# Second expert team's gather spread over the first team's steps from rows with a pool of their own, and router logits in column tiles with a summing product

## Chip, core and metric

One core of a Trainium2 chip. The metric is the device time of one execution in microseconds (us), the median of three runs. The trace is one execution taken by the hardware profiler. Its engines are PE (TensorE matmuls; PEld their weight loads), DVE (VectorE), ACT (ScalarE), POOL (GpSimd) and SP (SyncE, whose queue issues nearly all loads).

## What is computed

A trunk of two layers over 256 positions of width 1024, all in float32. Each layer has four token mixers side by side, then a channel mixer: a dense SwiGLU in layer 0, and in layer 1 eight experts of which each position uses two. The change touches only this last stage:

```python
def moe_ffn(h, router_w, w1, w3, w2):
    logits = (h @ router_w).astype(jnp.float32)
    top_vals, top_idx = lax.top_k(logits, TOP_K)
    top_w = jax.nn.softmax(top_vals, axis=-1)
    gate = jnp.sum(jax.nn.one_hot(top_idx, N_EXPERTS) * top_w[..., None], axis=-2)
    out = jnp.zeros_like(h)
    for e in range(N_EXPERTS):
        out = out + gate[..., e:e + 1] * swiglu(h, w1[e], w3[e], w2[e])
    return out
```

The result goes through a residual sum and a final RMSNorm. The experts' three weight arrays together are 277 MB in float32, and all of it is read.

## The kernel before

A plan is a Python list; `run` (line 192) walks it and emits instructions in its order. A scheduler may then move an instruction ahead of its neighbours on its engine where it waits for nothing, except the matmuls of `tiles` and `warm`, which keep their program order.

**The expert stage.** Experts form two teams of four. Each expert has 64 slots (CAP) for positions, and a team has two reserves of 32 slots, FULL, for experts that are chosen more often. `route` (line 1275) normalises the rows, transposes them into `hT_moe`, multiplies by the router weights `rw` (line 1293: two halves of the positions, eight products each, the stationary operand a 128x128 block of `hT_moe`, the moving one 8 columns), copies the logits to `lg` (line 1295), and finds the two best experts and each position's slot in a chain of small DVE operations. `rows_in_parts` (line 1389) splits the normalised rows into `hh` and `hl`, two float32r parts. `gather(s)` (line 1444) then makes the team's input `X` by multiplying the parts with a 0/1 matrix `pm`: eight chunks of four matmuls (line 1454) for the 256 slots, and `gather_extra` (line 1461) eight chunks of four narrow matmuls (line 1468) for the reserves.

**Weights come in steps.** One step is one k (128 rows of a weight matrix) of four experts: a 2 MB load (1.5 MB for the last columns) into a tile named `quad`. A team has 70 steps: for each of three column blocks (`COLS`) eight of w1 and eight of w3, then 22 of w2. `use` and `round_` (line 1530) consume a step with five calls of `tiles` (line 315), each call four products that stand in four 32-column tiles of the PE array; the first four calls read the `quad`, the fifth reads `own`, a copy of two experts' weights that DVE and ACT make (lines 1526, 1527). In the trace each float32 product is two MATMUL records, so a step is 40 of them.

**Buffers.** Loads are issued on SP's queue in order, each when a place is free. There are four places "A", opened during the last projection of the mixers, one "B", opened when the expert stage begins, and two "first" (FIRST), which are used once and not given back. The five others are given back when their step has been read. So the first seven steps are loaded ahead; load 7 waits for step 0 (load 8 for step 1, and so on to load 11 for step 4), and load 12 waits for step 7, as steps 5 and 6 used the "first" places. (Steps and loads are counted from 0.)

**Side work.** Generators (`Side`, line 126) emit pieces of other work between the calls of `tiles`. What a generator yields sets how long it waits: 1500 units times the number, or 700 for 0, on a planner's count `now` (`tick`, line 253) that each call of `tiles` raises by 858. `finish` steps all active generators until the named one has ended. After step 6 `then` (line 1646) frees the "first" places, makes the second team's `pm`, and starts its gather (`both(1)`, which yields 0 between chunks) and `spread(0)` (line 1476: 12 matmuls of one column, three pairs of transposes). The tiles `hh` and `hl` use four of the five buffers of the tag "g" in the stage's own pool; `silu` (line 1567) needs two of these for the first team's activations. So `use` ends the second team's gather in step 7 (`finish(st["gather", 1])`), before the first `silu`, and then starts `spread(1)`.

Of the kernel before, what the change touches and what calls it, by code (L numbers as in the profile page):

```python
# [10 lines left out]
F32 = mybir.dt.float32  # L11
F32R = mybir.dt.float32r
# [128 lines left out]
class Trunk:  # L141
# [218 lines left out]
    def load_tables(self):  # L360
        nc, a = self.nc, self.a
        n0 = C_OFFS["ident"][1]
        nc.sync.dma_start(self.keep[:, n0:], a["consts"][:, n0:C_KEEP])
        nc.sync.dma_start(self.mixk[:, :C_LATE - C_KEEP], a["consts"][:, C_KEEP:C_LATE])
        rows = self.mixc.tile([102, P], F32, name="rows")
        r = lambda n, pat: a[n].rearrange(pat, p=P)
        nc.sync.dma_start(rows[0:48], r("ssd_conv_w", "l k (b p) -> (l k b) p"))
        nc.sync.dma_start(rows[48:60], r("ssd_conv_b", "l (b p) -> (l b) p"))
        nc.sync.dma_start(rows[60:92], r("ml_conv_w", "l k (b p) -> (l k b) p"))
        nc.sync.dma_start(rows[92:100], r("ml_conv_b", "l (b p) -> (l b) p"))  # L370
        nc.sync.dma_start(rows[100:102], r("gla_b_alpha", "l (b p) -> (l b) p"))
        self.bc = self.mixc.tile([P, 5, L, 4], F32, name="bc")
        for i, n in enumerate(("ssd_dt_bias", "ml_b_i", "ml_b_f", "ssd_a_log", "ssd_d")):
            nc.sync.dma_start(self.bc[:, i], _bcast(a[n], [[4, L], [1, 4]]))
        self.walpha = self.mixc.tile([16, L, P], F32, name="walpha")
        nc.sync.dma_start(self.walpha, a["gla_w_alpha"].rearrange("l r c -> r l c"))
        self.rows = rows
        self.ranks = self.const.tile([P, 2 * P], F32R, name="ranks")
        for i, n in enumerate(("tris", "ones")):
            nc.gpsimd.tensor_scalar(self.ranks[:, i * P:(i + 1) * P], self.c(n), 1.0, None, op0=OP.mult)  # L380
        self.rw = self.const.tile([P, KT, NE], F32, name="rw")
        nc.sync.dma_start(self.rw, a["router_w"][0].rearrange("(k p) e -> p k e", p=P))

    def load_narrow(self, l):

# [889 lines left out]
    def route(self, l):  # L1275
# [8 lines left out]
        self.load_gain("final_norm_g", 0)  # L1284
        hT = early("hT_moe").rearrange("p (k s) -> p k s", k=KT)
        self.turned(h, lambda q, t, pt: nc.scalar.activation(hT[:, q, t], pt, AF.Copy))
        self.rows_in_parts(h)
        nc.scalar.dma_start(self.kept.rearrange("p (a d) -> p a d", a=2), h)
        pl = self.psum()
        lg = T((P, 2, NE), "lg")  # L1290
        for t in range(2):
            for k in range(KT):
                nc.tensor.matmul(pl[:, t * NE:(t + 1) * NE], hT[:, k, t * P:(t + 1) * P], self.rw[:, k],
                                 start=k == 0, stop=k == KT - 1)
        nc.vector.tensor_copy(lg, pl[:, :2 * NE].rearrange("p (t e) -> p t e", t=2))
        self.warm(6)


# [87 lines left out]
            pool.tensor_tensor(gate, ohs[0], ohs[1], op=OP.add)  # L1386
        self.later = later

    def rows_in_parts(self, h):

        self.hh, self.hl = [[self.mp.tile([P, D], F32R, tag="g", bufs=GS, name=f"{n}{self.num()}")
                             for _ in range(2)] for n in ("hh", "hl")]
        for t in range(2):
            self.nc.scalar.activation(self.hh[t], h[:, t], AF.Copy)
            (self.nc.vector, self.nc.gpsimd)[t].tensor_tensor(self.hl[t], h[:, t], self.hh[t].bitcast(F32),
                                                              op=OP.subtract)

    def experts(self, l, n, first):
# [42 lines left out]
                                            st["zo"][:, t, :, s, None].to_broadcast([P, FULL, SUB]),  # L1441
                                            iota[:, None, 1:1 + SUB].to_broadcast([P, FULL, SUB]), op=OP.is_equal)

        def gather(s):

            pm = st["pm", s]
            X = st["X", s] = T((P, KT, WIDE), f"X{s}", pool=self.late if s else self.mp)
            rows = [(self.hh[0], 0), (self.hh[1], 1), (self.hl[0], 0), (self.hl[1], 1)]
            yield 1
            for k in range(KT):  # L1450
                pt = self.psum((P, SLOTS))
                ks = slice(k * P, (k + 1) * P)
                for i, (src, t) in enumerate(rows):
                    nc.tensor.matmul(pt, src[:, ks], pm[:, t, :SLOTS], start=i == 0, stop=i == 3)  # L1454
                yield 0
                if k % 2:
                    nc.vector.tensor_copy(X[:, k, :SLOTS], pt)
                else:
                    nc.scalar.activation(X[:, k, :SLOTS], pt, AF.Copy)

        def gather_extra(s):
            pm, X = st["pm", s], st["X", s]
            rows = [(self.hh[0], 0), (self.hh[1], 1), (self.hl[0], 0), (self.hl[1], 1)]
            pt = self.psum((P, KT, FULL * SUB))
            for k in range(KT):
                ks = slice(k * P, (k + 1) * P)
                for i, (src, t) in enumerate(rows):
                    nc.tensor.matmul(pt[:, k], src[:, ks], pm[:, t, SLOTS:WIDE], start=i == 0, stop=i == 3)  # L1468
                yield 0
            nc.vector.tensor_copy(X[:, :, SLOTS:], pt)  # L1470

        def both(s):
            yield from gather(s)
            yield from gather_extra(s)

        def spread(s):

# [62 lines left out]
        def up(s, ci):  # L1540
            c0, n_ = COLS[ci]
            w_2 = n_ // 2
            got = {}

            def use(w_, k, raw):
                if k == 0:
                    if w_ + ci == 0:
                        self.finish(st["gather", s])
                    got[w_] = {key: self.psum()[:, :w_2] for key in
                               [(h, r) for h in range(2) for r in range(ROUNDS)] + ["full"]}  # L1550
                round_(got[w_], st["X", s][:, k], raw, pick(s, raw, n_), w_2, k == 0, k == KT - 1)
                if k == KT - 1:
                    if s + ci + w_ == 0:
                        self.finish(st["gather", 1])
                        go("spread", 1, spread(1))
                    st["act", s, ci, w_] = sd = Side((silu, act)[w_](s, ci, got))
                    self.spawn(sd)
            return [Step(w[k, :, s * TEAM:(s + 1) * TEAM, c0:c0 + n_], n_, lambda raw, w_=w_, k=k: use(w_, k, raw))
                    for w_, w in enumerate((w1, w3)) for k in range(KT)]
# [13 lines left out]
        def act(s, ci, got):  # L1573
            w = COLS[ci][1] // 2
            nb = w // P
            gT = st["gT", s, ci] = T((P, 8, WIDE), "gT", 3, pool=self.late)
            for key, gv in halves(s, ci):
                nc.vector.tensor_mul(gv, gv, got[1][key])
            for key, gv in halves(s, ci):
# [55 lines left out]
        def go(name, s, gen):  # L1635
            st[name, s] = sd = Side(gen)
            self.spawn(sd)
# [8 lines left out]
        def then():  # L1646
            if first:
                self.early.close()
                self.late = self.pool("late")
            hot(1)  # L1650
            hot_extra(1)
            go("gather", 1, both(1))
            go("spread", 0, spread(0))

        for s in range(TEAMS):
            for ci in range(len(COLS)):
                steps = up(s, ci)
                if s + ci == 0:
                    at = WEIGHTS + 1 + FIRST
                    steps.insert(at, then)  # L1660
                plan += steps
            plan.append(lambda s=s: self.finish(st["spread", s]))
            if s == 0 and n == 0:
                plan.append(self.shares_left)
            plan += down(s)
        return plan

    def moe(self, l):
        def begin():
            self.cutting.close()  # L1670
            self.homes["B"] = self.pool("quad", side="right"), 1
            self.mp = self.pool("moe")
            self.early = ExitStack()
            self.soon = self.pool("soon", ctx=self.early)
            self.homes["first"] = self.soon, FIRST
            self.places.extend(["B"] + ["first"] * FIRST)
        return self.experts(l, 0, [begin, "fetch", lambda: self.route(l)])

    def shares_left(self):

# [4 lines left out]
    def moe_rest(self, l, n=1):  # L1685

        most = self.nc.values_load(self.shares[n - 1]["most"][0:1, 0:1], min_val=0, max_val=S)
        with self.tc.If(most > 0):
            self.nc.vector.tensor_tensor(self.slot, self.slot, self.shares[n - 1]["done"][:, None, :].to_broadcast(
                [P, 2, NE]), op=OP.subtract)  # L1690
            again = self.late.tile([P, 8, WIDE], F32, tag="gT", bufs=3, name=f"again{n}")
            again = again.rearrange("p a b -> p (a b)")[:, :2048]
            self.nc.sync.dma_start(again, self.kept)
            self.rows_in_parts(again.rearrange("p (a d) -> p a d", a=2))
            self.run(self.experts(l, n, None))
            if n + 1 < PASSES:
                self.moe_rest(l, n + 1)
# [3 lines left out]
    def final(self):  # L1701
        nc = self.nc
        g = self.gains["final_norm_g", 0]
        y = self.late.tile([P, 8, WIDE], F32, tag="gT", bufs=3, name=f"rows{self.num()}").rearrange("p a b -> p (a b)")[:, :2048]
        y = self.norm(g, y.rearrange("p (a d) -> p a d", a=2))
        ov = self.out.rearrange("o (t p) d -> p (o t) d", p=P)
        for t in range(2):
# [45 lines left out]
```

## Time and profile before

| | |
|---|---|
| Median of 3 runs (lowest, highest) | 1474.21 us (1472.54, 1474.55) |
| The profiled execution: its own time | 1472.85 us |
| Its span in the trace (first to last instruction) | 1471.1 us |
| Busy in the span: PE, DVE, ACT, POOL | 94%, 42%, 36%, 13% |
| Moved by DMA | 404 MB, 275 GB/s mean |

The first 750 us are the mixers and the dense layer. The expert stage takes the rest. PE counts as busy in nearly all slices of the span, which says little: matmuls are pipelined and their ends are modelled. How fast the weights come, and which wait ends last, is read stage by stage below. "PEclk" is the granted TensorE clock, 1.00 for 2.4 GHz and 0.50 for 1.2 GHz.

### The profile page before, as it was taken

The page shows a single profiled execution, that of the slowest core. Times are in us where ns is not written, and L with a number is a line of the kernel's source. Part 1 is how long each engine was busy: PE and PEld are TensorE (multiplying, and loading weights), DVE is VectorE, ACT ScalarE, POOL GpSimd, SP SyncE. Part 2 cuts the span into 40 slices and gives each one's busy share as a digit, 9 for nine tenths or more (in the row PEclk, how much of TensorE's full clock was granted, in tenths as well). Part 3 has the DMA queues.
Part 4 walks back from the last instruction along what each step waited for, and adds up shares of the span by engine and source line. Part 5 has one row for each costly group of instructions (what it writes and reads, how often), then busy time and mean ns, then how long its engine had stood idle before and what let it go on. Part 6 is the DMA issues. An engine that isn't in the chain of part 4 may idle for free.

```text
span 1471.1 us, 26423 instructions
## 1 busy us (share of the span) xinstructions
PE 1381.0 (94%) x11170; PEld 901.7 (61%) x11170; DVE 611.9 (42%) x1069; ACT 534.9 (36%) x717; POOL 185.5 (13%) x211
## 2 busy tenths in 40 slices
PE   7999999999999999999999999988889998998886
PEld 6888999799998888999983432322223222232222
DVE  5876555655545786555553221212113121212113
ACT  5643444444444553344432222222223222232222
POOL 0366211100000318322210000000000000000000
PEclk9999999999999999999989999999999999999999
DMA  8735366675552432636687699999999999999993
GB/s 249 260 117 156 112 190 202 195 262 179 194 184 74 159 115 87 201 117 198 240 319 287 252 409 409 400 399 408 408 409 409 408 409 408 402 397 406 408 408 146
DMA packets 182458, 404.26 MB, mean 275 GB/s; under 512 B 12470, under 2 KB 95804, under 8 KB 182076
## 3 DMA queue, kind: packets, MB, share of 16 engines
q1 hardware_dynamic: 181612, 400.34, 74.1%
q8 instruction: 89, 1.46, 0.4%
q10 hardware_dynamic: 720, 2.16, 0.4%
q14 instruction: 37, 0.30, 0.1%
HBM read 400.39 MB, written 2.10 MB: 274 GB/s over the span
## 4 chain that ended last, share of the span: by engine, by line
PE 57%; DMA 33%; DVE 5%; POOL 2%; ACT 1%; issue 1%; SPq 1%; POOLq 0%; ACTq 0%; DVEq 0%
DMA quad<-in_moe_w_dram 32%; PE ps L309 13%; PE ps L310 12%; PE ps L311 12%; PE ps L319 12%; DVE lo L304 2%; PE ps L529 1%; PE ps L1627 1%; PE ps L1454 1%; ACT hi L303 1%; DMA raw<-in_w_in_dram 1%; DVE xbc L579 1%; DMA mixk<-in_consts_dram 1%; PE ps L1583 0%; PE ps L1468 0%
## 5 line engine op out<-in xcount | busy, mean ns | idle before, releaser
L319 PE MATMUL ps<-quad,X 128*32 128x512 f32 (+1 forms) x3072 | 325.7, 561 | 28.4 <-DMA quad<-in_moe_w_dram 28.4
L304 DVE TENSOR_TENSOR lo<-raw,hi 128x1024 fp32r<-128x1024 f32 x222 | 277.3, 1254 | 167.3 <-ACT hi L303 167.0
L309 PE MATMUL ps<-hThi,hi 128*128 128x256 f32 x1120 | 319.8, 286 | 0.0
L311 PE MATMUL ps<-hTlo,hi 128*128 128x256 f32 x1120 | 314.8, 281 | 0.4 <-DVE hTlo L304 0.4
L310 PE MATMUL ps<-hThi,lo 128*128 128x256 f32 x1120 | 314.9, 281 | 0.0
L303 ACT ACTIVATE hi<-raw 128x1024 fp32r<-128x1024 f32 x222 | 232.9, 1056 | 204.9 <-PE ps L311 114.1
L1526 DVE COPY own<-quad 128x1024 f32 (+1 forms) x140 | 92.7, 663 | 510.1 <-DMA quad<-in_moe_w_dram 432.1
L1527 ACT ACTIVATE own<-quad 128x1024 f32 (+1 forms) x140 | 141.3, 1010 | 447.5 <-DMA quad<-in_moe_w_dram 372.6
L319 PEld LDWEIGHTS ps<-quad,X 128*32 128x32 f32 x3072 | 93.8, 110 | 236.8 <-issue 169.3
L309 PEld LDWEIGHTS ps<-hThi,hi 128*128 128x128 f32 x1120 | 212.3, 190 | 2.9 <-issue 0.7
L310 PEld LDWEIGHTS ps<-hThi,lo 128*128 128x128 f32 x1120 | 211.8, 189 | 0.6
L311 PEld LDWEIGHTS ps<-hTlo,hi 128*128 128x128 f32 x1120 | 211.6, 189 | 0.6 <-DVE hTlo L304 0.6
L319 PE MATMUL ps<-quad,gT 128*32 128x512 f32 x1408 | 160.5, 595 | 27.6 <-DMA quad<-in_moe_w_dram 27.6
L319 PEld LDWEIGHTS ps<-quad,gT 128*32 128x32 f32 x1408 | 41.6, 109 | 142.4 <-issue 84.4
L423 POOL TENSOR_TENSOR rstd<-rs,mhalf 128x1 f32<-128x1 f32 x10 | 5.5, 556 | 881.0 <-DVE rs L419 864.0
L319 PE MATMUL ps<-own,X 128*32 128x512 f32 (+1 forms) x768 | 93.4, 558 | 0.0
L1110 POOL TENSOR_TENSOR m<-m 128x512 f32<-128x512 f32 x16 | 34.7, 2171 | 152.2 <-DVE m L1108 137.4
L319 PEld LDWEIGHTS ps<-own,X 128*32 128x32 f32 x768 | 24.5, 110 | 47.7 <-issue 44.8
L309 PE MATMUL ps<-hi,hThi 128*128 128x512 f32 (+1 forms) x128 | 51.6, 405 | 0.0
L311 PE MATMUL ps<-lo,hThi 128*128 128x512 f32 (+1 forms) x128 | 47.8, 374 | 0.7 <-DVE lo L304 0.7
L310 PE MATMUL ps<-hi,hTlo 128*128 128x512 f32 (+1 forms) x128 | 48.2, 377 | 0.0
L319 PE MATMUL ps<-own,gT 128*32 128x512 f32 x352 | 45.9, 593 | 0.0
(332 smaller groups left out, 1480.8 us busy)
## 6 DMA issues: line engine op xcount, KB each, us to landing
quad<-in_moe_w_dram SPq DMA_DIRECT2D x108, 2048.0 KB, 20.9
raw<-in_w_in_dram SPq DMA_DIRECT2D x62, 1024.0 KB, 5.4
quad<-in_moe_w_dram SPq DMA_DIRECT2D x32, 1536.0 KB, 16.9
raw<-in_ffn_w_dram SPq DMA_DIRECT2D x33, 1024.0 KB, 5.4
raw<-in_w_branch_dram SPq DMA_DIRECT2D x8, 1024.0 KB, 5.3
raw<-in_w_out_dram SPq DMA_DIRECT2D x8, 1024.0 KB, 5.1
mixk<-in_consts_dram SPq DMA_DIRECT2D x1, 1536.0 KB, 15.3
x<-in_x_dram SPq DMA_DIRECT2D x2, 512.0 KB, 5.0
```

The costliest lines, as they stand in the source:

```text
L303: nc.scalar.activation(hi, src, AF.Copy)
L304: nc.vector.tensor_sub(lo, src, hi.bitcast(F32))
L309: mm(out, ah, bh, start=start, stop=False)
L310: mm(out, al, bh, start=False, stop=False)
L311: mm(out, ah, bl, start=False, stop=stop)
L319: ins = self.nc.tensor.matmul(outs[gs], a, b, start=start, stop=stop, tile_position=(0, SUB * g))
L529: nc.tensor.matmul(pt[:, :256], k[:, :P], q, start=True, stop=True)
L579: nc.vector.scalar_tensor_tensor(o[:, d:], pt[:, u, :S - d], tap(3 - d), o[:, d:], op0=OP.mult, op1=OP.add)
L1110: nc.gpsimd.tensor_tensor(m[:, 0:2], m[:, 0:2], m[:, 2:4], op=OP.add)
L1454: nc.tensor.matmul(pt, src[:, ks], pm[:, t, :SLOTS], start=i == 0, stop=i == 3)
L1526: nc.vector.tensor_copy(own[:, 0:1, :n_], raw[:, bass.ds(v0, 1)])
L1527: nc.scalar.activation(own[:, 1:2, :n_], raw[:, bass.ds(v1, 1)], AF.Copy)
```

## The change

- `rw` is padded with zeros to 32 columns per k (a POOL memset ahead of its load), and `sums`, a 128x8 matrix with a one where the row modulo 32 equals the column, is made on POOL from the identity.
- In `route`, the logits are formed in column tiles: two calls of `tiles` with the padded `rw` as stationary operands (32 columns) and 256 columns of `hT_moe` as moving operand, four k in each call, so that a 128x256 PSUM tile holds four partial sums. DVE copies it to SBUF (`logits`), and two products with `sums` add the four parts and turn the result.
- `hh` and `hl` get a pool of their own ("rows", on the right side), so the tag "g" is free of them. In later passes over the experts, run only where an expert's positions do not fit, they lie in the tag "gT".
- The two "first" places are opened after the logits, in the region of the normalised rows and `hT_moe`; their two loads are issued after `route` and no longer at the stage's start.
- The second team's gather yields 3 between chunks (4500 units) and no longer 0. It is ended not in step 7 but after step 23 (`then_rows`, in the second column block), where the pool "rows" is closed and `spread(1)` starts. The tag "gT" has one buffer in "late" and two in "lasts", which takes the place of "rows".

```diff
@@ -378,8 +378,14 @@
         self.ranks = self.const.tile([P, 2 * P], F32R, name="ranks")
         for i, n in enumerate(("tris", "ones")):
             nc.gpsimd.tensor_scalar(self.ranks[:, i * P:(i + 1) * P], self.c(n), 1.0, None, op0=OP.mult)
-        self.rw = self.const.tile([P, KT, NE], F32, name="rw")
-        nc.sync.dma_start(self.rw, a["router_w"][0].rearrange("(k p) e -> p k e", p=P))
+        self.rw = self.const.tile([P, KT, SUB], F32, name="rw")
+        nc.gpsimd.memset(self.rw, 0.0)
+        nc.sync.dma_start(self.rw[:, :, :NE], a["router_w"][0].rearrange("(k p) e -> p k e", p=P))
+        self.sums = self.const.tile([P, NE], F32, name="sums")
+        ident = self.c("ident")
+        nc.gpsimd.tensor_tensor(self.sums, ident[:, 0:NE], ident[:, SUB:SUB + NE], op=OP.add)
+        for g in range(2, TEAM):
+            nc.gpsimd.tensor_tensor(self.sums, self.sums, ident[:, g * SUB:g * SUB + NE], op=OP.add)
 
     def load_narrow(self, l):
 
@@ -1284,15 +1290,22 @@
         self.load_gain("final_norm_g", 0)
         hT = early("hT_moe").rearrange("p (k s) -> p k s", k=KT)
         self.turned(h, lambda q, t, pt: nc.scalar.activation(hT[:, q, t], pt, AF.Copy))
-        self.rows_in_parts(h)
+        self.rows_in_parts(h, True)
         nc.scalar.dma_start(self.kept.rearrange("p (a d) -> p a d", a=2), h)
-        pl = self.psum()
         lg = T((P, 2, NE), "lg")
+        part, pl = self.psum((P, S)), self.psum()
+        for k0 in range(0, KT, TEAM):
+            self.tiles(part, [self.rw[:, k0 + g] for g in range(TEAM)], [hT[:, k0 + g] for g in range(TEAM)],
+                       k0 == 0, k0 == KT - TEAM)
+        logits = T((P, S), "logits")
+        nc.vector.tensor_copy(logits, part)
         for t in range(2):
-            for k in range(KT):
-                nc.tensor.matmul(pl[:, t * NE:(t + 1) * NE], hT[:, k, t * P:(t + 1) * P], self.rw[:, k],
-                                 start=k == 0, stop=k == KT - 1)
+            nc.tensor.matmul(pl[:, t * NE:(t + 1) * NE], logits[:, t * P:(t + 1) * P], self.sums, start=True, stop=True)
         nc.vector.tensor_copy(lg, pl[:, :2 * NE].rearrange("p (t e) -> p t e", t=2))
+        self.early.close()
+        self.early = ExitStack()
+        self.homes["first"] = self.pool("first", ctx=self.early), FIRST
+        self.places.extend(["first"] * FIRST)
         self.warm(6)
 
 
@@ -1386,10 +1399,15 @@
             pool.tensor_tensor(gate, ohs[0], ohs[1], op=OP.add)
         self.later = later
 
-    def rows_in_parts(self, h):
-
-        self.hh, self.hl = [[self.mp.tile([P, D], F32R, tag="g", bufs=GS, name=f"{n}{self.num()}")
-                             for _ in range(2)] for n in ("hh", "hl")]
+    def rows_in_parts(self, h, first):
+
+        if first:
+            self.rows = ExitStack()
+            pool = self.pool("rows", side="right", ctx=self.rows)
+            both = [pool.tile([P, 2 * D], F32R, name=n) for n in ("hh", "hl")]
+        else:
+            both = [self.lasts.tile([P, 8 * WIDE], F32R, tag="gT", bufs=2, name=f"{n}{self.num()}") for n in ("hh", "hl")]
+        self.hh, self.hl = [[t_[:, t * D:(t + 1) * D] for t in range(2)] for t_ in both]
         for t in range(2):
             self.nc.scalar.activation(self.hh[t], h[:, t], AF.Copy)
             (self.nc.vector, self.nc.gpsimd)[t].tensor_tensor(self.hl[t], h[:, t], self.hh[t].bitcast(F32),
@@ -1441,7 +1459,7 @@
                                             st["zo"][:, t, :, s, None].to_broadcast([P, FULL, SUB]),
                                             iota[:, None, 1:1 + SUB].to_broadcast([P, FULL, SUB]), op=OP.is_equal)
 
-        def gather(s):
+        def gather(s, pace):
 
             pm = st["pm", s]
             X = st["X", s] = T((P, KT, WIDE), f"X{s}", pool=self.late if s else self.mp)
@@ -1452,13 +1470,13 @@
                 ks = slice(k * P, (k + 1) * P)
                 for i, (src, t) in enumerate(rows):
                     nc.tensor.matmul(pt, src[:, ks], pm[:, t, :SLOTS], start=i == 0, stop=i == 3)
-                yield 0
+                yield pace
                 if k % 2:
                     nc.vector.tensor_copy(X[:, k, :SLOTS], pt)
                 else:
                     nc.scalar.activation(X[:, k, :SLOTS], pt, AF.Copy)
 
-        def gather_extra(s):
+        def gather_extra(s, pace):
             pm, X = st["pm", s], st["X", s]
             rows = [(self.hh[0], 0), (self.hh[1], 1), (self.hl[0], 0), (self.hl[1], 1)]
             pt = self.psum((P, KT, FULL * SUB))
@@ -1466,12 +1484,12 @@
                 ks = slice(k * P, (k + 1) * P)
                 for i, (src, t) in enumerate(rows):
                     nc.tensor.matmul(pt[:, k], src[:, ks], pm[:, t, SLOTS:WIDE], start=i == 0, stop=i == 3)
-                yield 0
+                yield pace
             nc.vector.tensor_copy(X[:, :, SLOTS:], pt)
 
-        def both(s):
-            yield from gather(s)
-            yield from gather_extra(s)
+        def both(s, pace=0):
+            yield from gather(s, pace)
+            yield from gather_extra(s, pace)
 
         def spread(s):
 
@@ -1550,9 +1568,6 @@
                                [(h, r) for h in range(2) for r in range(ROUNDS)] + ["full"]}
                 round_(got[w_], st["X", s][:, k], raw, pick(s, raw, n_), w_2, k == 0, k == KT - 1)
                 if k == KT - 1:
-                    if s + ci + w_ == 0:
-                        self.finish(st["gather", 1])
-                        go("spread", 1, spread(1))
                     st["act", s, ci, w_] = sd = Side((silu, act)[w_](s, ci, got))
                     self.spawn(sd)
             return [Step(w[k, :, s * TEAM:(s + 1) * TEAM, c0:c0 + n_], n_, lambda raw, w_=w_, k=k: use(w_, k, raw))
@@ -1573,7 +1588,7 @@
         def act(s, ci, got):
             w = COLS[ci][1] // 2
             nb = w // P
-            gT = st["gT", s, ci] = T((P, 8, WIDE), "gT", 3, pool=self.late)
+            gT = st["gT", s, ci] = T((P, 8, WIDE), "gT", 2 if ci else 1, pool=self.lasts if ci else self.late)
             for key, gv in halves(s, ci):
                 nc.vector.tensor_mul(gv, gv, got[1][key])
             for key, gv in halves(s, ci):
@@ -1649,15 +1664,23 @@
                 self.late = self.pool("late")
             hot(1)
             hot_extra(1)
-            go("gather", 1, both(1))
+            go("gather", 1, both(1, 3))
             go("spread", 0, spread(0))
+
+        def then_rows():
+            self.finish(st["gather", 1])
+            if first:
+                self.rows.close()
+                self.lasts = self.pool("lasts", side="right")
+            go("spread", 1, spread(1))
 
         for s in range(TEAMS):
             for ci in range(len(COLS)):
                 steps = up(s, ci)
                 if s + ci == 0:
-                    at = WEIGHTS + 1 + FIRST
-                    steps.insert(at, then)
+                    steps.insert(WEIGHTS + 1 + FIRST, then)
+                if s == 0 and ci == 1:
+                    steps.insert(KT, then_rows)
                 plan += steps
             plan.append(lambda s=s: self.finish(st["spread", s]))
             if s == 0 and n == 0:
@@ -1672,9 +1695,8 @@
             self.mp = self.pool("moe")
             self.early = ExitStack()
             self.soon = self.pool("soon", ctx=self.early)
-            self.homes["first"] = self.soon, FIRST
-            self.places.extend(["B"] + ["first"] * FIRST)
-        return self.experts(l, 0, [begin, "fetch", lambda: self.route(l)])
+            self.places.append("B")
+        return self.experts(l, 0, [begin, "fetch", lambda: self.route(l), "fetch"])
 
     def shares_left(self):
 
@@ -1688,10 +1710,10 @@
         with self.tc.If(most > 0):
             self.nc.vector.tensor_tensor(self.slot, self.slot, self.shares[n - 1]["done"][:, None, :].to_broadcast(
                 [P, 2, NE]), op=OP.subtract)
-            again = self.late.tile([P, 8, WIDE], F32, tag="gT", bufs=3, name=f"again{n}")
+            again = self.late.tile([P, 8, WIDE], F32, tag="gT", bufs=1, name=f"again{n}")
             again = again.rearrange("p a b -> p (a b)")[:, :2048]
             self.nc.sync.dma_start(again, self.kept)
-            self.rows_in_parts(again.rearrange("p (a d) -> p a d", a=2))
+            self.rows_in_parts(again.rearrange("p (a d) -> p a d", a=2), False)
             self.run(self.experts(l, n, None))
             if n + 1 < PASSES:
                 self.moe_rest(l, n + 1)
@@ -1701,7 +1723,7 @@
     def final(self):
         nc = self.nc
         g = self.gains["final_norm_g", 0]
-        y = self.late.tile([P, 8, WIDE], F32, tag="gT", bufs=3, name=f"rows{self.num()}").rearrange("p a b -> p (a b)")[:, :2048]
+        y = self.late.tile([P, 8, WIDE], F32, tag="gT", bufs=1, name=f"out_rows{self.num()}").rearrange("p a b -> p (a b)")[:, :2048]
         y = self.norm(g, y.rearrange("p (a d) -> p a d", a=2))
         ov = self.out.rearrange("o (t p) d -> p (o t) d", p=P)
         for t in range(2):
```

## Rows read from the trace of the kernel before

**Rows 1.** The page's chain that ended last, shares of the span by line.

```profile
DMA quad<-in_moe_w_dram 32%; PE ps L309 13%; PE ps L310 12%; PE ps L311 12%; PE ps L319 12%; DVE lo L304 2%; PE ps L529 1%; PE ps L1627 1%; PE ps L1454 1%; ACT hi L303 1%; DMA raw<-in_w_in_dram 1%; DVE xbc L579 1%; DMA mixk<-in_consts_dram 1%; PE ps L1583 0%; PE ps L1468 0%
```

**Rows 2.** The same chain in order of time, 860 us on: start, us, what.

```profile
870.05 37.95 PE ps L319 x352
...
908.07 21.10 DMA quad<-in_moe_w_dram
...
1450.88 4.50 PE ps L319 x40
```

**Rows 3.** Stretches: us, busy PE, PEld, DVE, ACT, POOL; PEclk, DMA share, GB/s.

```profile
769.00:778.40 9.40, 9.40 (x90) 6.07 (x93) 8.50 (x54) 2.81 (x5) 0.00 (x0) 1.00 0.05 12
778.40:805.20 26.80, 26.80 (x256) 7.94 (x246) 7.00 (x27) 7.17 (x7) 1.05 (x2) 1.00 1.00 388
805.20:810.20 5.00, 5.00 (x41) 2.83 (x37) 0.42 (x1) 1.03 (x3) 0.00 (x0) 1.00 0.11 30
...
815.80:825.30 9.50, 9.50 (x71) 5.46 (x70) 1.09 (x2) 2.06 (x4) 0.00 (x0) 0.82 0.06 9
...
832.20:857.20 25.00, 25.00 (x236) 7.54 (x232) 6.63 (x12) 6.01 (x6) 0.00 (x0) 1.00 1.00 384
...
908.00:1450.00 542.00, 486.58 (x4602) 149.50 (x4594) 95.28 (x146) 138.55 (x167) 0.00 (x0) 1.00 1.02 402
```

**Rows 4.** Timeline of SP's queue: loads 7, 12 and 13 issued.

```profile
777.29 0.37 SPq L272 DMA_DIRECT2D quad<-in_moe_w_dram  x1
...
808.93 0.37 SPq L272 DMA_DIRECT2D quad<-in_moe_w_dram  x1
...
824.11 0.37 SPq L272 DMA_DIRECT2D quad<-in_moe_w_dram  x1
```

**Rows 5.** The chain in order of time, 770 to 870 us.

```profile
773.60 31.89 PE ps L319 x296
805.50 0.67 PE ps L1454 x4
806.17 0.99 PE ps L319 x8
...
809.50 1.23 PE ps L1497 x12
...
815.25 3.49 PE ps L1468 x32
818.74 5.27 PE ps L319 x32
...
829.51 0.37 PE ps L1504 x2
...
859.71 0.59 PE ps L1583 x4
```

**Rows 6.** Timeline of all engines, router: start, us, instruction, [idle before].

```profile
753.05 1.26 ACT L1286 ACTIVATE hT_moe<-ps 128x512 f32<-128x512 f32 x2 [0.37 <-PE ps L459]
...
753.51 6.10 PE L1293 MATMUL ps<-rw,hT_moe 128*128 128x8 f32 x32
...
759.65 0.18 DVE L1295 COPY lg<-ps 128x16 f32<-128x16 f32 x1 [5.55 <-PE ps L1293]
```

**Rows 7.** Groups by form, 773 to 860 us: busy us, mean ns.

```profile
L319 PEld LDWEIGHTS ps<-quad,X 128*32 128x32 f32 x528 | 16.8, 112 | 37.5 <-issue 36.6 <-PE ps L319 0.6
...
L1457 DVE COPY X<-ps 128x256 f32<-128x256 f32 x4 | 1.7, 423 | 3.7 <-PE ps L1454 3.6
```

**Rows 8.** Stretches at a lower clock, columns as in rows 3.

```profile
754.00:767.70 13.70, 12.75 (x54) 11.50 (x54) 5.27 (x30) 1.90 (x5) 3.67 (x7) 0.51 1.01 393
818.70:824.20 5.50, 5.50 (x36) 1.50 (x35) 0.69 (x1) 1.81 (x4) 0.00 (x0) 0.69 0.00 0
```

**Rows 9.** Start of the kernel: POOL's timeline, then SP's.

```profile
20.10 1.06 POOL L380 TENSOR_SCALAR ranks<-keep 128x128 fp32r<-128x128 f32 x2 [9.34 <-DMA keep<-in_consts_dram]
...
22.57 0.42 SPq L382 DMA_DIRECT2D rw<-in_router_w_dram  x1
```

## The prediction

> **What bounds the kernel now.** I read the chain that ended last first. Its largest single part is the loads of the expert weights, 32% of the span [rows 1]. In order of time, PE carries the chain up to 908.07 us; from there the chain is one load of expert weights after another, PE waiting 21.10 us in the first merged piece, until the last step's products begin at 1450.88 [rows 2]. The stretch 908 to 1450 shows a DMA share of 1.02 at 402 GB/s, PE busy 486.58 of 542 us [rows 3]. A load of 2.097 MB thus takes 5.22 us, a step on PE 4.31 us (296 records in 31.89 us, 40 to a step [rows 5]). So this end is set by how many bytes have come by a given time, and only an earlier or fuller weight stream moves it.
>
> Next I looked for places where the stream stands still, and cut the time there into stretches. After the seven loads that have a place ahead, DMA is nearly empty from 769.0 to 778.4 (12 GB/s): load 7 goes out only at 777.29, when step 0 has been read [rows 3, 4]. It is full until 805.2, at 30 GB/s until 810.2, stands at 9 GB/s from 815.8 to 825.3, and is full again from 832.2 [rows 3]. Load 12 goes out at 808.93, load 13 at 824.11 [rows 4]: each waits for PE to finish a step, and PE then did other things than steps. The chain shows them: the gather's chunks of 0.67 us at line 1454, then 32 narrow products at line 1468 in one piece of 3.49 us, then four tile calls (32 records) in 5.27 us instead of 4 x 0.86 [rows 5], with the clock at 0.69 on average there [rows 8]. That is the second team's gather, ended by force in step 7.
>
> **Part 1, the logits.** Removed: 32 records of 8 columns, 6.10 us [rows 6]. They end in `lg` at 759.65. All of `hT_moe` is there at 753.05 + 1.26 = 754.31 [rows 6]; the old products began before that on the first half of the positions, the new ones need both halves. Added: two tile calls of 256 columns. A call of 512 takes 0.86 us, so 0.43 each at the full clock; this stretch ran at 0.51 [rows 8], so I take 0.86 each, the first partly before 754.31: end at about 755.4. Then a DVE copy of 128x256 out of PSUM, 0.42 us [rows 7] plus some 0.2 for the hand-over: 756.0. Then two float32 products with a 128x128 stationary part, four records at 6.10/32 = 0.19, with a first latency of some 0.3: 757.1. `lg` then starts near 757.2, 2.4 us earlier. Everything to step 0 hangs on `lg` in one chain of small operations, so step 0 moves by the same 2.4. Bounds: 3.6 earlier if the clock is full there and the gather behind it gains too; 0.4 earlier if the six warming products behind the logits are scheduled ahead of the two sums, while these wait for the copy.
>
> Here a rule stands against the change. The row: weight loads of the tile calls take 112 ns each [rows 7], eight to a call, 0.90 us, yet a whole call with its four 512-column products takes 0.86 us [rows 5]; so they run beside the products. The Trainium skill (TensorE: Matmul & The Clock Gate, Part 3, section "The mechanism") says that a weight load overlaps running products only where its row group differs; column tiles share all rows. By that rule the two calls would cost 2 x 0.90 more, and the gain would be 0.6 and not 2.4. The trace disagrees, and I go by the row.
>
> The zero padding and `sums` are on POOL at the start. The `rw` load waits for the memset; behind it on SP stand the gain and the first projections' loads, which are needed soon. It goes out at 22.57, POOL is done with `ranks` at 20.10 + 1.06 = 21.16 [rows 9]; a memset of 256 columns between them fits. Cost zero; if it came 1 us later, up to that 1 us.
>
> The "first" loads now wait for the logits, the split into `hh`, `hl` and the store of the rows; with the logits' products done at 757 I estimate 758 to 760. Two loads of 5.22 us are done by 771, while load 7 is not issued before 775 and step 5 reads the first of them at about 793. Cover: DMA's empty stretch to 778.4 [rows 3]. Without it each us of delay beyond 764 would push load 7.
>
> **Part 2, the gather.** In time from step 0 (773.60). Before: loads 7 to 11 are in at 31.6; DMA empty 5.0; load 12; empty 9.5 [rows 3]; load 13, some 6 us to 831.3 (load 12 took 5.6, 810.2 to 815.8); empty 0.9 up to 832.2; together 15.4 us. After: step 7 still begins at 7 x 4.3 = 30.1. A chunk costs 0.67, and the next tile call 0.13 more (0.99 for 0.86 [rows 5]), so 0.80. Pace 3 asks for 4500 units, six calls of 858: one chunk in 1.2 steps. Step 7 holds one chunk, so its `quad` is read at 30.1 + 3.4 + 0.8 = 34.3, and load 12 starts 1.3 later (808.93 to 810.2 [rows 3, 4]) at 35.6: empty 4.0. It ends at 40.8. Step 7 also holds the spread's 12 products (1.23 + 0.13), so step 8 begins at 36.6; with a chunk and two transposes (0.37 + 0.13 each) its `quad` is read at 41.8, load 13 starts at 43.1: empty 2.3. Step 9 begins at 43.2, is read at 46.6 to 47.4, and load 14 can start at 47.9 to 48.7 against 48.3, when load 13 ends. From there a PE step takes 4.3 + 0.80/1.2 = 4.97 against 5.22: the stream is full. Empty 6.3 instead of 15.4: 9.1 us.
>
> Against it stands what PE must still do before step 26: sixteen chunks (8 x 0.80, 8 x (3.49/8 + 0.13)), two spreads of 2.9, and the transposes of the first activations (five of 0.59 + 0.13), 20.3 us over 18 steps. With 18 x 4.31 that is 97.9, against 94.0 at 5.22 us for a load, or 98.3 at the 384 GB/s of 832.2 to 857.2 [rows 3]. So PE may be the slower one by 0 to 3.9 us; I take 1.0. Gain 8.1 of the 9.1. The copies out of PSUM that move along are on DVE and ACT, each 0.4 us to a step; idle time there covers them. The gather holds one of eight PSUM banks throughout; five are a step's sums, and the activations empty theirs as each call ends, so I count nothing.
>
> **The sum.** 1472.85 (the profiled execution's own time, 1.75 above its span) less 2.4 less 8.1 is 1462.3. That execution is 1.36 below the median of the runs, so against the median: 1474.2 - 10.5 = 1463.7. A measurement of this kernel can tell about 0.2%, 2.9 us, from no change, so "same" ends at 1471.3.
>
> **Rivals.** (a) PE has too little slack: the 3.9 us are lost in full, and the logits bring 1 us; 1474.2 - 9.1 + 3.9 - 1.0 = 1468.0. For it: 97.9 against 94.0. Against: the last eight chunks are partly left to step 24, when five loads stand ahead. 0.17.
> (b) Weight loads of column tiles don't overlap: 1465.5, inside the forecast's range; against it [rows 5, 7]. 0.04.
> (c) The gather isn't spread after all: another `finish` or the scheduler draws the chunks together in steps 7 and 8. Only the logits remain: 1471.8. Against: between step 7 and step 23 nothing in the plan ends a generator. 0.06.
> (d) Slower: the clock. It fell to half after the narrow products of the forced gather, 0.69 over 818.7 to 824.2, and was 0.51 around the router [rows 8]. If the mixture of chunks and tile calls lets it fall for long, a step costs 2 x 4.97 = 9.9 against 5.22, 4.7 us lost per step; from the third such step the gain of 10.5 is gone. With five: 1463.7 + 23.5 = 1487. Against: tile calls with transposes in between ran at 1.00 from 832.2 on [rows 3]. 0.06.
> (e) More than forecast: the stream keeps full from load 12 on and the router keeps its clock: 1474.2 - 11.4 - 3.6 = 1459.2. 0.09.
> The forecast itself, 1460.5 to 1466.5: 0.58.
>
> **How the numbers follow.** The range of 1458.8 to 1469.5 takes in (e), the forecast, (b) and (a), 0.88 together less the edges of (a) and (e), and leaves out (c) and (d). Faster by over 0.2%: 0.58 + 0.17 + 0.04 + 0.09 = 0.88. Same: (c), 0.06. Slower: (d), 0.06.
>
> **What would show it.** Right: `lg` about 2 us earlier counted from `hT_moe`; loads 12 and 13 issued some 34 and 42 us after step 0 (35.3 and 50.5 before); no DMA stretch emptier than 4 us behind load 7; chunks of line 1454 at every sixth tile call to step 23; narrow products in the second column block. Wrong: a load later than these that starts late again, above all for steps 16 to 26; half clock beyond 780 us; a "first" load that lands after step 5 could begin; SP waiting for POOL near 22 us.

## The result

| | before | after |
|---|---|---|
| Median us (lowest, highest; runs) | 1473.45 (1472.54, 1474.55; 4) | 1460.80 (1460.41, 1463.92; 4) |
| Ratio, 95% interval | | 0.9918 [0.9901, 0.9936] |
| Profiled execution, its span | 1472.85, 1471.1 | 1460.79, 1458.9 |

The changed kernel is 12.1 us faster by the ratio; 1463.7 was forecast, in a range of 1458.8 to 1469.5. The line numbers of the changed kernel are 13 to 22 higher behind `route`.

The page's chain that ended last, shares by line, of the changed kernel; it answers to [rows 1]:

```profile
DMA quad<-in_moe_w_dram 27%; PE ps L319 17%; PE ps L309 13%; PE ps L310 13%; PE ps L311 13%; DVE lo L304 1%; PE ps L535 1%; PE ps L1642 1%; PE ps L1472 1%; ACT hi L303 1%; PE ps L1598 1%; PE ps L1486 1%; DMA mixk<-in_consts_dram 1%; PE ps L545 0%; PE ps L546 0%
```

Five points of the chain went from the loads (32 to 27) to the tile calls of line 319 (12 to 17). In order of time (start, us, what):

```profile
770.37 31.89 PE ps L319 x296
802.27 0.67 PE ps L1472 x4
802.93 1.85 PE ps L319 x16
804.79 1.43 PE ps L1515 x12
...
817.65 5.29 PE ps L319 x48
822.93 0.67 PE ps L1472 x4
823.60 5.29 PE ps L319 x48
...
970.30 15.73 DMA quad<-in_moe_w_dram
...
1438.80 4.50 PE ps L319 x40
```

Step 0 begins at 770.37, 3.23 us earlier than in [rows 5]. A chunk of the gather (0.67) now stands behind every sixth tile call (48 records). The chain first passes to a load at 970.30 and not at 908.07 [rows 2]; the last step begins at 1438.80, 12.08 earlier. The tail behind it is the same within 0.1 us. A piece of the chain that names a load is the time from the load's issue to its landing. PE itself stands still for only part of it, in the changed kernel for the first time just ahead of

```profile
980.96 2.79 PE L319 MATMUL ps<-quad,X 128*32 128x384 f32 x32 [0.45 <-DMA quad<-in_moe_w_dram]
```

and before just ahead of 913.86, for 0.63 us.

Stretches of the changed kernel, columns as in [rows 3]:

```profile
754.00:761.90 7.90, 4.09 (x28) 2.88 (x29) 5.20 (x24) 1.02 (x2) 2.98 (x4) 1.00 0.58 208
761.90:765.40 3.50, 3.50 (x19) 3.50 (x18) 3.03 (x22) 0.77 (x2) 1.12 (x4) 0.51 0.99 386
772.10:775.30 3.20, 3.20 (x36) 0.98 (x32) 2.96 (x28) 0.39 (x1) 0.00 (x0) 1.00 0.16 32
775.30:801.80 26.50, 26.50 (x252) 7.93 (x244) 7.19 (x29) 7.08 (x8) 1.05 (x2) 1.00 1.00 389
801.80:805.90 4.10, 4.10 (x39) 2.13 (x31) 0.00 (x0) 3.64 (x6) 0.00 (x0) 1.00 0.10 39
805.90:811.90 6.00, 6.00 (x51) 2.28 (x55) 2.04 (x5) 1.54 (x2) 0.00 (x0) 1.00 0.94 343
811.90:813.70 1.80, 1.80 (x18) 0.49 (x14) 0.54 (x1) 0.54 (x1) 0.00 (x0) 1.00 0.28 64
813.70:860.00 46.30, 46.30 (x404) 15.72 (x396) 11.04 (x19) 12.41 (x16) 0.00 (x0) 1.00 1.01 394
```

The gaps behind load 7 are 4.1 and 1.8 us, 5.9 together; before they were 15.4 [rows 3]. From 813.7 the stream is full, where it was full from 832.2. The clock, at 0.51 from 754.0 to 767.7 before [rows 8], is at half only from 761.9 to 765.4.

Loads on SP's queue: the two "first" places, then loads 7, 12 and 13, to compare with [rows 4].

```profile
760.15 0.95 SPq L272 DMA_DIRECT2D quad<-in_moe_w_dram  x2
...
774.04 0.37 SPq L272 DMA_DIRECT2D quad<-in_moe_w_dram  x1
...
804.90 0.37 SPq L272 DMA_DIRECT2D quad<-in_moe_w_dram  x1
...
812.29 0.37 SPq L272 DMA_DIRECT2D quad<-in_moe_w_dram  x1
```

Counted from step 0, load 12 goes out at 34.5 us and load 13 at 41.9; before it was 35.3 and 50.5. The router's rows of the changed kernel:

```profile
752.62 1.26 ACT L1292 ACTIVATE hT_moe<-ps 128x512 f32<-128x512 f32 x2 [0.31 <-PE ps L465]
...
753.26 0.16 PEld L319 LDWEIGHTS ps<-hT_moe,rw 128*32 128x32 f32 x8 [0.26 <-ACT hT_moe L1292]
753.27 1.30 PE L319 MATMUL ps<-hT_moe,rw 128*32 128x256 f32 x16
...
753.92 0.16 PEld L319 LDWEIGHTS ps<-hT_moe,rw 128*32 128x32 f32 x8 [0.50 <-ACT hT_moe L1292]
...
754.63 0.42 DVE L1301 COPY logits<-ps 128x256 f32<-128x256 f32 x1 [0.97 <-PE ps L319]
...
754.90 2.38 POOL L1413 TENSOR_TENSOR hl<-h_moe,hh 128x1024 fp32r<-128x1024 f32 x1 [3.81 <-ACT hh L1412]
...
755.11 0.61 PE L1303 MATMUL ps<-sums,logits 128*128 128x8 f32 x4 [0.55 <-DVE logits L1301]
...
755.76 0.18 DVE L1304 COPY lg<-ps 128x16 f32<-128x16 f32 x1 [0.70 <-PE ps L1303]
...
756.18 1.13 DVE L1323 TENSOR_TENSOR c<-lg,m 128x16 f32<-128x16 f32 x1
```

From the end of `hT_moe` (753.88) to `lg` it takes 1.88 us, before 5.34 [rows 6]: 3.46 less. The second tile call waits for the end of `hT_moe` (its weight loads begin at 753.92), so the 1.30 us of the two calls hold a wait. The comparison at line 1323 takes 1.13 us, where its second execution (758.38) takes 0.18; more on it below.

### The profile page after: what moved, and what is told of

Read it like the earlier page. It is cut to its first block, busy times and chain, and to the rows that moved or that the text cites. A ratio compares the mean times of both kernels' runs of the same rounds, so it can differ in the third digit from the quotient of the medians.

```text
span 1458.9 us, 26399 instructions
## 1 busy us (share of the span) xinstructions
PE 1376.5 (94%) x11158; PEld 897.1 (61%) x11158; DVE 612.9 (42%) x1070; ACT 534.5 (37%) x717; POOL 187.9 (13%) x215
## 3 DMA queue, kind: packets, MB, share of 16 engines
q8 instruction: 89, 1.46, 0.4%
## 4 chain that ended last, share of the span: by engine, by line
PE 62%; DMA 28%; DVE 4%; POOL 2%; issue 1%; ACT 1%; SPq 1%; POOLq 0%; DVEq 0%; ACTq 0%
DMA quad<-in_moe_w_dram 27%; PE ps L319 17%; PE ps L309 13%; PE ps L310 13%; PE ps L311 13%; DVE lo L304 1%; PE ps L535 1%; PE ps L1642 1%; PE ps L1472 1%; ACT hi L303 1%; PE ps L1598 1%; PE ps L1486 1%; DMA mixk<-in_consts_dram 1%; PE ps L545 0%; PE ps L546 0%
```

## The experiments

Each was timed against the kernel before on the same chip; the ratios are comparable, the medians of before differ by up to 2 us between the groups.

| | median us | ratio to before, 95% interval |
|---|---|---|
| changed kernel | 1460.80 | 0.9918 [0.9901, 0.9936] |
| logits alone | 1469.12 | 0.9978 [0.9967, 0.9988] |
| gather alone | 1464.45 | 0.9943 [0.9928, 0.9958] |
| pace 0 | 1466.10 | 0.9955 [0.9941, 0.9968] |
| wide chunks four times | 1474.73 | 1.0015 [1.0002, 1.0028] |
| spreads in the w2 steps | 1457.23 | 0.9895 [0.9878, 0.9911] |
| the same, gather three steps later | 1455.92 | 0.9901 [0.9881, 0.9922] |
| the same, a sixth place | 1449.78 | 0.9840 [0.9823, 0.9857] |
| subtraction in four | 1460.41 | 0.9921 [0.9909, 0.9934] |

**The two parts by themselves.** Logits alone: the kernel before with the new lines for `rw`, `sums` and the logits, all else as it was.

> The kernel before with only the logits changed (padded rw, column tiles, summing product). Theory: everything to step 0 hangs on the logits, and the weight stream follows step 0, so the 3.2 to 3.5 us by which the logits come earlier in the changed kernel's trace arrive at the end: 1470.0 (1469.0 to 1471.3), lg about 3.5 us earlier counted from hT_moe. Rival: the stream's empty stretches swallow it, since they are set by the forced gather: 1473.4, no change.

Gather alone: the changed kernel with the old `rw` and the old loop:

```diff
-        for k0 in range(0, KT, TEAM):
-            self.tiles(part, ...)
+        for t in range(2):
+            for k in range(KT):
+                nc.tensor.matmul(pl[:, t * NE:(t + 1) * NE], hT[:, k, t * P:(t + 1) * P], self.rw[:, k],
+                                 start=k == 0, stop=k == KT - 1)
```

> The changed kernel with the old logits (32 records of 8 columns). Theory: the empty stretches behind load 12 are gone, 9 us of the gain, and the 3.3 us of the logits are missing: 1464.2 (1463.0 to 1465.5). Rival: the two parts overlap and the logits' share is hidden behind the stream: 1461, as the changed kernel.

By the ratios the logits bring 0.22% and the gather 0.57%, 3.2 and 8.4 us; together 0.79% against 0.82% measured for both (by the medians 4.6 and 9.3 against 12.7 us). They add up within the noise, and neither rival holds: the logits' share reaches the end, and it is not hidden behind the stream.

How much of it is the logits' own, one trace can't say. In the profiled execution of the logits alone step 0 begins at 771.28, 2.32 us earlier than before. The four tile calls behind the forced narrow products take

```profile
816.42 3.57 PE ps L319 x32
```

where they took 5.27 in [rows 5]: the clock, 0.69 on average over 818.7 to 824.2 before [rows 8], is 1.00 here, and these calls take 1.70 us less. No run shows whether this follows from the new logits or only from the execution.

**Pace or forced end?** The gather yields 0 between its chunks again, but is still ended only behind step 23.

```diff
-            go("gather", 1, both(1, 3))
+            go("gather", 1, both(1))
```

> The changed kernel, the second team's gather yielding 0 again and not 3 between chunks, still ended only behind step 23: sixteen chunks in steps 7 to 10, one behind each tile call. Theory: what counts is that a step on PE stays shorter than a load; with five chunks in a step it is 8 us, loads 12 to 15 go out late, and the stream stands for 6 to 8 us more: 1467 to 1469. Rival: the loss before came from the forced end alone (silu waiting for buffers of the tag g, the half clock behind the narrow products), so the pace is without effect: 1461.

0.37% slower than the changed kernel, 5.4 us: a little under the forecast, and not the rival's zero. The chain of this kernel, in order of time, has a chunk behind every tile call:

```profile
809.47 0.99 PE ps L319 x8
810.47 0.68 PE ps L1472 x4
811.15 0.22 PE ps L1522 x2
811.36 1.00 PE ps L319 x8
812.36 0.68 PE ps L1472 x4
```

and its stretches (columns as in [rows 3]) show the stream at 250 GB/s for 23.6 us behind the gap ahead of load 12:

```profile
802.40:806.40 4.00, 4.00 (x32) 1.95 (x29) 0.42 (x1) 3.21 (x6) 0.00 (x0) 1.00 0.05 19
806.40:830.00 23.60, 23.60 (x184) 11.05 (x186) 5.73 (x12) 4.97 (x8) 0.00 (x0) 1.00 0.69 250
```

PE's work to the end of the gather is the same, and PE never idles in it. So what the pace saves is stream time: a load can go out only when a step has been read, and steps of 8 us leave it nothing to do. The remaining 3 us between this run and the logits alone I put down to the end forced in step 7 and its place; no run shows that apart.

**How much room has PE?** The four products of each wide chunk of the second team are issued four times over; the sums of the first three rounds are not used.

```diff
-                for i, (src, t) in enumerate(rows):
-                    nc.tensor.matmul(pt, src[:, ks], pm[:, t, :SLOTS], start=i == 0, stop=i == 3)
+                for again in range(4 if s else 1):
+                    for i, (src, t) in enumerate(rows):
+                        nc.tensor.matmul(pt, src[:, ks], pm[:, t, :SLOTS], start=i == 0, stop=i == 3)
```

> The changed kernel with the four products of each of the second team's eight wide chunks issued four times over (the last run's sums stay). Adds 8 x 3 x 0.46 = 11 us on PE in steps 7 to 16. Theory: PE has only some 0.25 us a step to spare there, so nearly all of it comes out at the end: 1469 to 1472. Rival: the weight stream is the bound from load 14 on and PE has room, since five loads stand ahead: 1461 to 1463.

None: 13.9 us above the changed kernel by the medians, more than was added. The chain in order of time:

```profile
771.83 34.60 PE ps L319 x296
806.42 2.09 PE ps L1473 x16
808.51 1.85 PE ps L319 x16
...
986.13 15.95 DMA quad<-in_moe_w_dram
```

A chunk takes 2.09 for 0.67, eight of them 11.4 us more. In this execution the first steps took 34.60 for 31.89, with the clock at 0.92 on average over them, and step 0 began 1.46 later: 15.5 together, and this execution took 1476.56 against 1460.79, 15.8 more. The chain first passes to a load at 986.13. So work that is added to PE ahead of that comes out at the end in full. It does so by way of the stream, which is not full here. The changed kernel first, then this run (columns as in [rows 3]):

```profile
806.00:876.00 70.00, 70.00 (x600) 23.86 (x600) 15.70 (x27) 18.21 (x23) 0.00 (x0) 1.00 0.98 374
...
806.00:876.00 70.00, 70.00 (x594) 32.02 (x590) 13.66 (x24) 18.46 (x24) 0.00 (x0) 1.00 0.82 302
```

A chunk of 2.09 to six tile calls of 5.29 makes a step of 6.15 us, longer than a load, and loads wait for places as they do with pace 0. The run shows that the changed kernel has no room for more work on PE. Whether less work would bring anything is left to the next run.

**Less of PE's work ahead of that wait.** Both spreads go into the w2 steps of their team:

```diff
-            go("spread", 0, spread(0))
...
-            go("spread", 1, spread(1))
...
-            plan.append(lambda s=s: self.finish(st["spread", s]))
...
-            plan += down(s)
+            steps = down(s)
+            steps.insert(len(steps) - 1, lambda s=s: self.finish(st["spread", s]))
+            steps.insert(4, lambda s=s: go("spread", s, spread(s)))
+            plan += steps
```

> The changed kernel with both spreads (2.9 us of PE each) moved from steps 7 to 9 and 24 to 26 into the w2 steps of their team (started behind the fourth, ended ahead of the last). Theory: from step 0 to about 970 us PE never waits, so work taken out of that stretch comes out of the end, until the stream itself has no gap left but the one ahead of load 12; in the w2 steps PE waits for loads and has the room: 1456 to 1458.5. Rival: the stream is the bound there already and the spreads are hidden: 1461.

As expected: 0.23% below the changed kernel, 3.4 us (3.6 by the medians; the two intervals overlap a little). The second gap is gone (columns as in [rows 3]), and the chain first passes to a load at 954.40, 15.9 us earlier than in the changed kernel:

```profile
801.60:805.60 4.00, 4.00 (x40) 1.58 (x40) 0.23 (x1) 3.73 (x7) 0.00 (x0) 1.00 0.13 33
805.60:860.00 54.40, 54.40 (x472) 18.66 (x468) 12.04 (x20) 15.70 (x21) 0.00 (x0) 1.00 1.01 394
...
954.40 15.43 DMA quad<-in_moe_w_dram
```

Some 5 to 6 us of work left that stretch of PE, and the profiled execution is 2.8 us shorter: 0.4 because step 0 began earlier, 1.9 for the gaps (4.0 against 5.9), and 0.5 besides. So work that is taken away from PE pays as far as it fills the stream, and no further: here the stream is the bound, not PE.

On top of it, the gather three steps later:

```diff
-            go("gather", 1, both(1, 3))
+        def start():
+            go("gather", 1, both(1, 3))
...
+                    steps.insert(10, start)
...
-                    steps.insert(KT, then_rows)
+                    steps.insert(2 * KT - 1, then_rows)
```

> As the run with the spreads in the w2 steps, and the second team's gather starts behind step 9, not step 6, and may run to step 30. Theory: step 7 without a chunk is read 0.8 us earlier, load 12 starts that much earlier, and the narrow chunks need no burst: 0.5 to 1 us below the run without it. Rival: only the sum of PE's work to 970 us counts, which is the same: no difference.

Inconclusive: 1.3 us less by the medians, 0.06% more by the ratios, and the intervals overlap almost wholly.

On top of the spreads instead, a sixth place:

```diff
-WEIGHTS, FIRST, GS = 4, 2, 5
+WEIGHTS, FIRST, GS = 4, 1, 4
...
+        self.homes["C"] = self.pool("more"), 1
-        self.places.extend(["first"] * FIRST)
+        self.places.extend(["C"] + ["first"] * FIRST)
...
-                    steps.insert(WEIGHTS + 1 + FIRST, then)
+                    steps.insert(WEIGHTS + 2 + FIRST, then)
...
-            own = T((P, FULL, 1024), "own", 2)
+            own = T((P, FULL, 1024), "own", 1)
...
-            pT = st["pT", s] = T((P, ROUNDS + 2, 2, P), "pT", 2, F32R, self.late)
+            pT = st["pT", s] = T((P, ROUNDS + 2, 2, P), "pT", 1, F32R, self.late)
```

> As the run with the spreads in the w2 steps, and one of the two places that are used once becomes a sixth lasting one (one buffer fewer each for own, pT and g makes the room). Theory: load 12 then goes out when step 5 is read, 8 us earlier, so the last gap of 4 us is gone: 3 to 4 us below the run without it, 1452.5 to 1455. Rival: PE, which still takes more than 4.9 us for a step with a chunk, becomes the bound, or own with one buffer makes DVE and ACT late for the fifth tile call: no gain or a loss, 1457 to 1465.

1449.78 us, 23 below the kernel before and some 7 to 8 below the five places: the fastest here, and more than the 3 to 4 us that were expected. Its stretches:

```profile
778.50:880.00 101.50, 101.50 (x896) 33.56 (x892) 19.23 (x32) 30.03 (x37) 0.00 (x0) 1.00 1.01 397
...
1000.00:1400.00 400.00, 365.98 (x3385) 112.03 (x3381) 73.47 (x117) 102.71 (x120) 0.52 (x1) 1.00 1.03 410
```

There is no gap from 778.5 on. That was to bring 4 us, but in this execution step 0 begins 0.7 us later than in the run without the place, and the first 296 records take 34.70 for 31.89, with the clock at 0.92 on average: some 0.5 us are left. The rest is the rate, 410 GB/s from 1000 to 1400 us. With five places and the spreads in w2 the same stretch has 407, as it has in the kernel before and in the changed kernel:

```profile
1000.00:1400.00 400.00, 363.06 (x3357) 110.94 (x3353) 72.69 (x116) 101.72 (x119) 0.00 (x0) 1.00 1.03 407
```

0.7% of the 600 us or so for which the stream is full is 4 us, with the rounding of the rates 3 to 6; the two profiled executions are 7.1 us apart. This run also has smaller buffers elsewhere, so that the place alone raises the rate is likely and not shown apart.

**The long comparison.** POOL's second subtraction in `rows_in_parts` in four pieces:

```diff
+            n_ = D // 4 if t and first else D
+            for c in range(0, D, n_):
+                cs = slice(c, c + n_)
-            (self.nc.vector, self.nc.gpsimd)[t].tensor_tensor(self.hl[t], h[:, t], ...
+                (self.nc.vector, self.nc.gpsimd)[t].tensor_tensor(self.hl[t][:, cs], h[:, t, cs], ...
```

> The changed kernel with POOL's subtraction that makes the second half of hl (2.38 us) cut into four pieces of 256 columns. In the changed kernel the first comparison of the router chain on DVE (line 1323, two inputs in SBUF) takes 1.13 us and ends 0.03 us behind that subtraction; before it took 0.17. Theory: the two exclude each other for the length of a POOL instruction, so with pieces of 0.6 us the comparison takes 0.6 us or less and step 0 comes 0.5 to 0.9 us earlier: 1459.8 to 1460.5. Rival: the length is the comparison's own (something it waits for in that place): it stays at 1.13 us and the time at 1460.8.

```profile
755.99 2.80 POOL L1416 TENSOR_TENSOR hl<-h_moe,hh 128x256 fp32r<-128x256 f32 x4 [3.81 <-ACT hh L1412]
...
757.27 0.17 DVE L1323 TENSOR_TENSOR c<-lg,m 128x16 f32<-128x16 f32 x1
...
757.48 0.66 DVE L1324 TENSOR_TENSOR c<-c,io 128x16 f32<-128x16 f32 x1
...
758.17 0.17 DVE L1325 TENSOR_REDUCE i<-c 128x2 f32<-128x16 f32 x1
...
758.38 0.45 DVE L1326 TENSOR_TENSOR oh<-io,i 128x16 f32<-128x16 f32 x1
```

The mechanism is right, the gain is not. The comparison takes 0.17 again, so its length was not its own; now two later operations wait, 0.49 and 0.28 us more than their 0.17, until about 758.8, when the pieces are done. The sum of the waits fell from 0.96 to 0.77, POOL took 0.42 longer, and the time is the same.

## Why the prediction was right

By the profiled executions 12.06 us were gained: step 0 came 3.23 earlier, the gaps behind load 7 shrank by 15.4 - 5.9 = 9.5, and 0.7 were lost later. The forecast's terms were 2.4, 9.1 and 1.0. The sum did not come right by errors that cancel: each term came out close, and each a little in the kernel's favour. Two parts may belong to the executions and not to the change: 0.43 because the stage began earlier, and the half clock of the forced gather before (1.70), which the logits-alone execution did not have.

- The logits: the mechanism held, the term was too small. Of its steps the clock was wrong: I took 0.86 us for a tile call at half clock, and the rows show 1.30 for both calls, a wait for `hT_moe` included, with the clock at 1.00 until 761.9. `lg` came 3.46 us earlier from `hT_moe`. Lost again were 0.66 between `lg` and step 0: the comparison that waits for POOL took 0.96, not in the forecast; before, POOL's subtraction was done by the time the router chain began. The stage itself began 0.43 earlier in this execution.
- Weight loads of column tiles: the prediction added up eight loads of 112 ns to 0.90 us for a call, and that reading was wrong. The loads stand side by side: the eight of a call take 0.16 us together (router's rows). Rival (b) would so have cost some 0.3 us and not 1.8, too little to be told by the time. The steps speak against it: there four loads take 0.13 us (775.48, below), and PE is without a gap from 775.3 to 801.8, as far as the modelled ends of its products tell, so the loads lie beside products. The Trainium skill (TensorE: Matmul & The Clock Gate, Part 3, "The mechanism") says that a weight load overlaps running products only where its row group differs; these rows, of column tiles that share all rows, do not agree with it.
- The gaps: 4.0 and 2.3 us forecast, 4.1 and 1.8 measured; load 12 at 34.5 and load 13 at 41.9 us after step 0, as written.
- PE's lack of slack, rival (a): 0 to 3.9 us were weighed, 1.0 taken, 0.7 came, as what is left over in the sum above. The trace has a place for it: from 858 to 876 the DMA share is 1.00 and yet the rate is 370 GB/s (below), where before it was 408 from 860 to 878. That PE has nothing to spare there for more work was right, as the chunks issued four times show. That it alone is the bound does not follow: 5 to 6 us less of its work gave 2.8 back, most of it the second gap.
- The bound: that the end hangs on the stream held. But the 21.10 us of [rows 2] are not PE's wait, as the prediction has it: PE stood still for 2.5 us of them, four times some 0.6. No term of the sum uses the 21.10. The load of 5.22 us is from a rate that takes in the stream's end; at 407 GB/s it is 5.15.
- Covers: the "first" loads went out at 760.15 (758 to 760 forecast), and DMA was empty again from 772.1 to 775.3, so they delayed nothing. The memset ahead of the `rw` load does not show: the stage began no later.
- Rivals (c) and (d) did not come: chunks stand behind every sixth tile call, and the clock is 1.00 through the gather in the profiled execution. A half clock in the first steps did appear in other kernels here, as a loss of 2.7 us.

The rows of the changed kernel for the second and the fourth of these points, a row of the timeline and a stretch:

```profile
775.48 0.13 PEld L319 LDWEIGHTS ps<-quad,X 128*32 128x32 f32 x4 [0.30 <-issue]
...
858.00:876.00 18.00, 18.00 (x160) 6.31 (x156) 2.08 (x3) 4.31 (x6) 0.00 (x0) 1.00 1.00 370
```

## What to carry to other kernels

Where a stream of loads has a fixed number of places, side work belongs between the steps in pieces that keep each step shorter than a load: the same work in a burst empties the stream, and time that the stream stands for want of a place is not made up. As long as PE never waits for a load, work that is added to it can come out in full; work that is taken from it pays only as far as it fills the stream. Read that from the GB/s and not from the DMA share alone, and put side work behind the first wait for a load. Count the places before anything else: one more here was worth more than moving both spreads.

## What was not expected

- DVE and POOL excluded each other: a comparison of 16 columns took 1.13 us and ended 0.03 us behind POOL's subtraction (754.90 + 2.38), in all runs with the new logits whose rows were read; cut in four, the waits moved to the next two-input operations, and the reductions in between kept their 0.17. The Trainium skill (SBUF — State Buffer, "SBUF: two separate sides") says that a DVE operation with two inputs in SBUF and a GpSimd operation that reads SBUF share a port pair that one holds for its whole instruction. The trace agrees.
- 402 GB/s was not the stream's limit. The 402 of [rows 3] take in the stream's end, where the last loads run out; from 1000 to 1400 us it is 407 with five places, in all four such kernels read, and 410 with six.
- The clock differs between executions in the first steps: 31.89 us for 296 records at 1.00, 34.60 and 34.70 in two other kernels with 0.92 on average over them. With the chunks issued four times these 2.7 us are needed to make up the 15.8 us at the end; for the sixth place nothing shows how much of them arrives.
